# Layer two of a two-layer attention trunk: one 640-column score run a tile, two exponentials a tile, and bias tables laid out on the host

## The chip, the cores and the metric

The kernel runs on one core of one Trainium2 chip. The metric is the device time of one launch in microseconds, given as the median of several runs. On this core TensorE (PE) does the matrix products, VectorE (DVE) and ScalarE (ACT) do elementwise work and read PSUM, GpSimd (POOL) does elementwise work in SBUF alone, and SyncE (SP) issues nearly all DMA transfers in one queue.

## The reference, cut to what matters

Two layers run over 1024 latent tokens (a grid of 16 rows and 64 columns) and 256 context tokens, width 1024, 16 heads of 64. Layer one is grouped-query attention over all tokens. Layer two, which the change is about, lets each token see a window of 8 rows by 16 columns with a learned relative bias, and all 256 context tokens without bias:

```python
s_nb = einsum('bqhd,bqkhd->bhqk', qr, kw) * ATTN_SCALE + bias      # 8 x 16 window
s_cx = einsum('bqhd,bshd->bhqs', qr, kc) * ATTN_SCALE               # 256 context tokens
p = softmax(concatenate([s_nb, s_cx], axis=-1))
o = einsum('bhqk,bqkhd->bqhd', p[..., :n_nb], vw) + einsum('bhqs,bshd->bqhd', p[..., n_nb:], vc)
yx = (o * silu(z)) @ w_out
```

The output is `rms_norm(x + g_x * yx)`. The matrix products have to be better than fp16, so nearly every operand is split into a high and a low fp16 part.

## The kernel before

Tokens are stored column by column of the grid, so a tile of 128 tokens is 8 grid columns of 16 rows, and the window of a query tile t lies in the key tiles t-1, t and t+1. There are 8 latent tiles (`NX`) and 2 context tiles (numbers 8 and 9).

Layer two runs over 8 pairs of heads, u = 0 to 7. For a pair, `b_load(u)` fetches and splits weights, `b_qk(u)` and `b_vz(u)` project (tiles `pb` and `pvz`, L1360 and L1393/L1396), and `b_att(u)` does the attention. The projections of pair u+1 are interleaved with the attention of pair u, so that PE has work while the softmax of a tile is under way. After the last pair only `b_out` (tile `pob`, L1566, the output projection and the final norm) is left to interleave.

For each half of the latent tiles and each head of the pair, `b_att` goes through the query tiles two at a time:

- For each of the two tiles, the scores against the 2 or 3 near key tiles go to a PSUM bank of tag `st` (tile `bsn`, L1424 and L1425: two matmuls, for the high and low part of q). One custom DVE instruction (L1444) adds the bias table, writes `bpf` in SBUF and takes the row maximum.
- The scores of both tiles against the 256 context tokens go to one bank of tag `mx` (tile `bsc`), and one DVE reduction (L1451) takes their maxima. L1453 joins the two maxima, L1454 negates them and adds a constant.
- ACT computes four exponentials a tile: near and context in fp16 (L1462 and L1463, into `bph`), and near and context again in fp32 with row sums (L1464 and L1465, into `bpf`). The context ones read PSUM, so the `mx` bank is held until ACT is done with both tiles.
- `p_split` (L1042 on DVE for each second tile, L1045 on POOL for the others) subtracts to get the low part, a DMA transposes high and low (L1468, tile `bpht`), and later PE multiplies by v (L1473 and L1475, tile `bpv`).
- `fin` normalises four tiles at a time: L1484 adds the two row sums, L1485 and L1486 scale and invert them, L1488 copies one half of `bpv` out, L1489 adds the other half, and four instructions of L1491 multiply by the inverse sum and by the gate.

The bias tables are built on the chip. At the start of the kernel's life 16 small DMAs copy slices of the bias into DRAM (`toe`, L1318), 8 more spread them over 128 partitions (`tabd`, L1321). `b_table(h)` then loads 3 blocks of 128 columns for a head and POOL adds row masks with three instructions (L1333 to L1335), giving five blocks, of which a tile uses two or three.

PSUM has 8 banks: tags `pj`, `pv`, `st` and `mx`, two each. The order of instructions on every engine is not the order of the code. A `Planner` (a list scheduler with costs written by hand) lays out all instructions of the program, refines its order five times, and fixes it. It treats a PSUM tile as one resource, whatever part of it an instruction touches. A change in one place therefore moves instructions elsewhere too.

Of the kernel before, what the change touches and what calls it, by code (L numbers as in the profile page):

```python
# [40 lines left out]
PFB, PHB, PTB = 5, 5, 8  # L41
# [460 lines left out]
def trunk_kernel(ctx, tc, x, cx, cc, norm_g, ng_row, b_cols, sel_c, w_mod, w_mod0, b_mod, a_qz, a_kv, a_qg, a_kg, a_w_out,  # L502
                 b_in, rpb, b_w_out, fin_g, cos_t, sin_t, mask_q, out):
# [750 lines left out]
    def a_out(t, halves=(0, 1), tag="st"):  # L1254
# [13 lines left out]
        for hf in halves:  # L1268
            ps = psum.tile([P, 512], F32, name=f"poa{t}{hf}", tag=tag, bufs=2)
# [45 lines left out]
    toe = dram.tile([GR, NH, 31, GR], F32, name="toe")  # L1315
    for r in range(GR):
        a = bass.AP(rpb.tensor, rpb.offset + 15 - r, [[31 * 31, NH], [31, 31], [1, GR]])
        DM.dma_start(toe[r], a)  # L1318
    tabd = dram.tile([P, NH, 384], F32, name="tabd")
    for c in range(8):  # L1320
        DM.dma_start(tabd[c * GR:(c + 1) * GR],  # L1321
                     toe.rearrange("r h e k -> r h (e k)")[:, :, (7 - c) * GR:(7 - c) * GR + 384])
# [4 lines left out]
    def b_table(h):  # L1327

        tb = bl.tile([P, 5, P], F32, name=f"tb{h}", tag="tb", bufs=2)
        tabs[h] = tb  # L1330
# [3 lines left out]
        G.tensor_tensor(tb[:, 4], tb[:, 3], mq[:, 1], op=ALU.add)
# [77 lines left out]
    def b_att(u):  # L1412
# [14 lines left out]
        for hf in range(2):  # L1427
            og = bl.tile([P, 4, P], F32, name=f"bog{u}{hf}", tag="og", bufs=2)
            for i in range(2):
                tq = tabs[2 * u + i]  # L1430
                pv = psum.tile([P, 4, P], F32, name=f"bpv{u}{i}{hf}", tag="pv", bufs=2)
                sums = bl.tile([P, 4, 2], F32, name=f"bsm{u}{i}{hf}", tag="sums", bufs=2)
                for t0 in (hf * 4, hf * 4 + 2):
                    nm = f"{u}{i}{t0}"
                    near = {t: range(max(0, t - 1), min(NX, t + 2)) for t in (t0, t0 + 1)}
                    mx = bl.tile([P, 2, 2], F32, name="bmx" + nm, tag="bmx", bufs=3)
                    pfs = {}
                    for t in (t0, t0 + 1):
# [5 lines left out]
                        V.tensor_tensor_reduce(pfs[t][:, 0:n], st[:, 0:n * P].rearrange("p (a b) -> p a b", b=P), tsel,  # L1444
                                               op0=ALU.add, op1=ALU.max, scale=1.0, scalar=-3.0e38,
                                               accum_out=mx[:, t - t0, 0:1])
# [4 lines left out]
                    V.tensor_reduce(mx[:, :, 1], sx, axis=AX.X, op=ALU.max)  # L1451
# [1 line left out]
                    V.tensor_reduce(nmx, mx, axis=AX.X, op=ALU.max)  # L1453
                    V.tensor_scalar(nmx, nmx, -1.0, CSH, op0=ALU.mult, op1=ALU.add)  # L1454
                    for t in (t0, t0 + 1):
                        n, j, pf = len(near[t]), t - t0, pfs[t]
                        k_ = n + 2
                        pp = bl.tile([P, 10, P], F16, name=f"bph{u}{i}{t}", tag="ph", bufs=PHB)
# [3 lines left out]
                        S.activation(ph[:, 0:n], pf[:, 0:n], AF.Exp, bias=m)  # L1462
                        S.activation(ph[:, n:n + 2], cx_, AF.Exp, bias=m)  # L1463
                        S.activation(pf[:, 0:n], pf[:, 0:n], AF.Exp, bias=m, accum_out=sums[:, t % 4, 0:1])  # L1464
                        S.activation(pf[:, n:n + 2], cx_, AF.Exp, bias=m, accum_out=sums[:, t % 4, 1:2])  # L1465
# [13 lines left out]
                        yield 625  # L1479

                def fin(pv=pv, sums=sums, og=og, i=i, hf=hf):
                    nm = f"{u}{i}{hf}"
# [1 line left out]
                    V.tensor_reduce(sm, sums, axis=AX.X, op=ALU.add)  # L1484
# [3 lines left out]
                    S.copy(oc, pv[:, :, HD:P])  # L1488
                    V.tensor_tensor(oc, pv[:, :, 0:HD], oc, op=ALU.add)  # L1489
                    for t in range(4):  # L1490
                        V.scalar_tensor_tensor(og[:, t, i * HD:(i + 1) * HD], oc[:, t], sm[:, t:t + 1],  # L1491
                                               sz[:, hf * 4 + t, i * HD:(i + 1) * HD], op0=ALU.mult, op1=ALU.mult)
# [54 lines left out]
    def b_out(t, tag):  # L1547
# [39 lines left out]
def _tables():  # L1587
# [9 lines left out]
    p = np.arange(P)  # L1597
    c_, r_ = p // GR, p % GR
    r0 = np.clip(r_ - 4, 0, 8)
    rowok = (r_[None, :] >= r0[:, None]) & (r_[None, :] < r0[:, None] + 8)  # L1600
    lt = c_[None, :] < c_[:, None]
    q = np.stack([rowok & ~lt, rowok, rowok & lt], 1)
    import ml_dtypes
    m = lambda b: np.where(b, 0.0, NEG).astype(ml_dtypes.bfloat16)
    return lay(c64), lay(s64), m(q)
# [53 lines left out]
```

## Time and profile before

| | |
|---|---|
| median of 3 runs | 1364.47 us (1362.18 to 1364.70) |
| profiled execution, own time | 1365.58 us |
| its span (first to last instruction) | 1363.8 us |
| PE busy | 1329.9 us, 98% of the span |
| DVE, ACT, POOL busy | 1003.1, 910.2, 664.7 us (74%, 67%, 49%) |
| layer one, roughly | 100 to 690 us |
| layer two's projections and attention | 766 to 1300 us, one pair about 62 us |
| granted TensorE clock | 0.999 |

A row of a window table gives, for a stretch of time, each engine's busy time with the count of its instructions, in the order PE, weight loads, DVE, ACT, POOL, and then the granted clock, the busy share of the DMA engines and GB/s. What is missing from a window's length in the PE column is time in which PE had nothing it could run. A row of a group table gives line, engine, operation, tiles and shape, the count, and then busy time, mean length of one in ns, and the idle time just before with what ended it.

### The profile page before, as it was taken

What the parts mean: (1) busy time and instruction counts of PE and PEld (TensorE: products, weight loads), DVE (VectorE), ACT (ScalarE), POOL (GpSimd) and SP (SyncE); (2) the same over time, 40 slices, a digit from 0 to 9 for tenths busy, and PEclk for the clock granted to TensorE, in tenths of its full rate; (3) what the DMA queues carried; (4) which work ended last, traced back from release to release, by engine and by line L of the source; (5) the groups of instructions that cost most, each with busy time, mean ns of one, the idle gap of its engine ahead of it and who ended that gap; (6) DMA issues with size and microseconds to landing.
All of it is one profiled execution on the core that took longest, in us unless ns stands there. A gap on an engine that the chain in (4) does not pass through costs nothing.

```text
span 1363.8 us, 34709 instructions
## 1 busy us (share of the span) xinstructions
PE 1329.9 (98%) x13183; PEld 927.6 (68%) x13183; DVE 1003.1 (74%) x2647; ACT 910.2 (67%) x2186; POOL 664.7 (49%) x855
## 2 busy tenths in 40 slices
PE   9999999999999999999999999999999999999897
PEld 6457777777777777776554486777768686867543
DVE  5788788878788789887276846777776867777743
ACT  3653788888787876878632437777776777786711
POOL 2573787777778775788743201312222222332332
PEclk9999999999999999999999999999999999999999
DMA  9652577878789777847066725666576656677932
GB/s 352 186 162 76 108 145 156 154 161 166 149 152 169 146 150 138 172 145 210 10 171 175 178 80 120 125 132 138 117 153 110 156 96 146 113 159 141 194 101 102
DMA packets 426959, 198.23 MB, mean 145 GB/s; under 512 B 382560, under 2 KB 389664, under 8 KB 426792
## 3 DMA queue, kind: packets, MB, share of 16 engines
q1 hardware_dynamic: 426216, 195.98, 65.3%
q8 instruction: 103, 1.69, 0.5%
q14 instruction: 64, 0.52, 0.1%
q10 hardware_dynamic: 576, 0.03, 0.0%
HBM read 90.51 MB, written 15.22 MB: 78 GB/s over the span
## 4 chain that ended last, share of the span: by engine, by line
PE 68%; DVE 11%; ACT 9%; DMA 5%; POOL 3%; issue 3%; SPq 1%; DVEq 0%; POOLq 0%; ACTq 0%
PE pa L946 11%; PE pb L1360 9%; PE pvz L1393 9%; PE poa L1275 7%; PE pob L1566 6%; PE st L1183 2%; PE st L1184 2%; PE pkv L817 2%; ACT bpf L1464 2%; PE pm L976 2%; PE bpv L1473 1%; PE pv L1052 1%; PE qpv L1104 1%; PE pv L1053 1%; PE pv L1051 1%
## 5 line engine op out<-in xcount | busy, mean ns | idle before, releaser
L1045 POOL TENSOR_TENSOR pl<-pf,ph 128x256 f16<-128x256 f32 x340 | 234.1, 714 | 58.2 <-ACT pf L1170 44.5
L1045 POOL TENSOR_TENSOR bph<-bpf,bph 128x256 f16<-128x256 f32 (+1 forms) x128 | 99.9, 790 | 319.5 <-ACT bpf L1464 256.3
L946 PE MATMUL pa<-wa,x 128*128 128x256 f16 x1536 | 213.4, 272 | 0.1
L1360 PE MATMUL pb<-hb_hi,wb 128*128 128x512 f16 (+1 forms) x640 | 193.3, 358 | 1.4 <-DVE bk L1379 1.0
L1393 PE MATMUL pvz<-wb,hb_hi 128*128 128x256 f16 x1024 | 175.4, 273 | 0.6 <-DVE bk L1379 0.3
L946 PEld LDWEIGHTS <-x 128*128 128x128 f16 x1536 | 143.2, 97 | 35.7 <-issue 1.3
L1168 ACT ACTIVATE ph<-st 128x512 f16<-128x512 f32 x200 | 119.1, 604 | 60.7 <-PE st L1184 50.0
L1360 PEld LDWEIGHTS <-wb 128*128 128x128 f16 x960 | 92.7, 98 | 72.5 <-issue 2.9
L1393 PE MATMUL pvz<-wb,hb_lo 128*128 128x256 f16 x512 | 139.6, 273 | 0.0
L1170 ACT ACTIVATE pf<-st 128x512 f32<-128x512 f32 x200 | 119.3, 609 | 1.7 <-POOL pl L1045 1.6
L977 DVE TENSOR_REDUCE mxp<-pm 128x1 f32<-128x512 f32 x160 | 107.9, 684 | 13.7 <-PE pm L976 12.3
L1045 POOL TENSOR_TENSOR qpp<-qpf,qpp 128x512 f16<-128x512 f32 x84 | 97.9, 1186 | 38.4 <-ACT qpf L1127 32.2
L1360 PE MATMUL pb<-hb_lo,wb 128*128 128x512 f16 (+1 forms) x320 | 114.4, 358 | 0.0
L1393 PEld LDWEIGHTS <-hb_hi 128*128 128x128 f16 x1024 | 97.1, 98 | 24.2 <-DVE bk L1379 1.1
L1051 PE MATMUL pv<-v,ph 128*128 128x65 f16 x800 | 104.0, 193 | 0.2 <-ACT ph L1168 0.2
L1052 PE MATMUL pv<-v,ph 128*128 128x64 f16 x800 | 104.0, 195 | 0.0
L1053 PE MATMUL pv<-v,pl 128*128 128x65 f16 x800 | 101.4, 192 | 0.5 <-POOL pl L1045 0.5
L1566 PE MATMUL pob<-wob,ob 128*128 128x512 f16 x384 | 86.7, 379 | 2.6 <-DVE bmx L1444 0.9
L1051 PEld LDWEIGHTS <-ph 128*128 128x128 f16 x800 | 75.8, 97 | 19.0 <-ACT ph L1168 0.7
L1462 ACT ACTIVATE bph<-bpf,bnx 128x384 f16<-128x384 f32 (+1 forms) x128 | 68.7, 582 | 27.2 <-DVE bnx L1454 27.1
L1052 PEld LDWEIGHTS <-ph 128*128 128x128 f16 x800 | 75.5, 97 | 12.6
L1053 PEld LDWEIGHTS <-pl 128*128 128x128 f16 x800 | 76.1, 99 | 10.5 <-POOL pl L1045 1.6
(272 smaller groups left out, 3812.1 us busy)
## 6 DMA issues: line engine op xcount, KB each, us to landing
wg<-in_w_mod SPq DMA_DIRECT2D x64, 256.0 KB
wsb<-in_b_in SPq DMA_DIRECT2D x64, 256.0 KB
wm<-in_w_mod SPq DMA_DIRECT2D x16, 512.0 KB
wsa<-in_a_qz SPq DMA_DIRECT2D x32, 256.0 KB
xstage<-in_x SPq DMA_DIRECT2D x8, 512.0 KB
wsoa<-in_a_w_out SPq DMA_DIRECT2D x16, 256.0 KB
x<-in_x SPq DMA_DIRECT2D x8, 512.0 KB
x_d<-x SPq DMA_DIRECT2D x8, 512.0 KB
```

The source lines that it names most:

```text
L946: T.matmul(ps[:, :, i, :], hA(a, kt, t), wt[w][:, kt, :], start=n == 0, stop=n == 3 * KT - 1)
L977: V.tensor_reduce(mxs[i][:, t, ch:ch + 1], pm, axis=AX.X, op=ALU.max)
L1045: G.tensor_tensor(lo[:, c], p32[:, c], hi[:, c], op=ALU.subtract)
L1051: T.matmul(pv[:, t, :], hi[:, c], v[:, 0:65], start=first and t == 0, stop=False)
L1052: T.matmul(pv[:, t, 0:HD], hi[:, c], v[:, 65:129], start=False, stop=False)
L1053: T.matmul(pv[:, t, :], lo[:, c], v[:, 0:65], start=False, stop=last and t == n - 1)
L1168: S.activation(ph, st, AF.Exp)
L1170: S.activation(p32, st, AF.Exp)
L1275: T.matmul(ps, lhs(a, kt), w[b][:, kt, :], start=n == 0, stop=n == 3 * KT - 1)
L1360: T.matmul(ps[:, 0:n].rearrange("p (t q) -> p t q", q=P), wt[a][:, kt, which * P:(which + 1) * P], hb[b][:, c0 // P:(c0 + n) // P, kt], st ...
L1393: T.matmul(ps[:, :, j, :], hb[a][:, t, kt], wt[w][:, kt, 256:512], start=m == 0, stop=m == 3 * KT - 1)
L1566: T.matmul(ps, ob[kt][:, t // 4, a, c], wout["b"][hf][b][:, kt, :], start=n == 0, stop=n == 3 * KT - 1)
```

## The change

The near and context scores of a query tile now lie side by side in one PSUM tile of two banks (tag `db`, two of them, in place of `st` and `mx`), 640 columns, or 512 at the two ends of the grid. One DVE instruction adds a table that also covers the context columns (zeros there) and takes the maximum of all of them. L1451 and L1453 are gone. ACT computes two exponentials a tile, both from SBUF. The row sums are one number a tile, so L1484 is gone, and the end of `fin` is two multiplications of all four tiles instead of four instructions; these now work in place in PSUM.

The tables come as an input `tab` with nine blocks a head, masks and context zeros included, laid out on the host; `near(t)` picks five (or four) of the nine. The DMAs of `toe`, `tabd` and the mask, and POOL's three additions a head are gone.

For tile 0 the blocks are in another order (near, context, context, near), so that its scores take three runs of columns instead of two. `st` and `mx` lie in a PSUM pool of their own which closes before layer two's attention; layer one keeps its tags. The last four tiles of `b_out` use the `db` tag: both halves of a tile's output lie in one two-bank tile. `PTB`, the buffers for transposed probabilities, goes from 8 to 7. The weights of the interleaving (320, 320, 625, 625 a pair of tiles) become 540, 540, 405, 405, with the same sum.

```diff
-PFB, PHB, PTB = 5, 5, 8
+PFB, PHB, PTB = 5, 5, 7
...
-    toe = dram.tile([GR, NH, 31, GR], F32, name="toe")
-    for r in range(GR):
...
-        DM.dma_start(toe[r], a)
-    tabd = dram.tile([P, NH, 384], F32, name="tabd")
-    for c in range(8):
-        DM.dma_start(tabd[c * GR:(c + 1) * GR],
...
     def b_table(h):
-        tb = bl.tile([P, 5, P], F32, name=f"tb{h}", tag="tb", bufs=2)
...
-        DM.dma_start(flat, tabd[:, h])
-        G.tensor_tensor(tb[:, 0], tb[:, 1], mq[:, 1], op=ALU.add)
-        G.tensor_tensor(tb[:, 4], tb[:, 3], mq[:, 1], op=ALU.add)
-        G.tensor_tensor(tb[:, 1:4], tb[:, 1:4], mq, op=ALU.add)
+        tabs[h] = bl.tile([P, 9, P], F32, name=f"tb{h}", tag="tb", bufs=2)
+        DM.dma_start(tabs[h].rearrange("p a b -> p (a b)"), tab[h])
+
+    def near(t):
+        if t == 0:
+            return (0, NX, NX + 1, 1), ((0, 0, 1), (P, NX, 2), (3 * P, 1, 1)), slice(2, 9, 2)
+        if t == NX - 1:
+            return (t - 1, t, NX, NX + 1), ((2 * P, t - 1, 2), (4 * P, NX, 2)), slice(0, 7, 2)
+        return (t - 1, t, t + 1, NX, NX + 1), ((P, t - 1, 3), (4 * P, NX, 2)), slice(1, 6)
...
-                        st = ps_st(f"bsn{u}{i}{t}")
-                        scores(st[:, 0:n * P], i, t, slice(near[t][0] * P, (near[t][-1] + 1) * P))
-                        V.tensor_tensor_reduce(pfs[t][:, 0:n], ..., tsel, ..., accum_out=mx[:, t - t0, 0:1])
-                        yield 320
-                    sx = ps_mx(f"bsc{nm}", shape=(P, 2, 256))
-                    for j in range(2):
-                        scores(sx[:, j, :], i, t0 + j, slice(NX * P, TOK))
-                    V.tensor_reduce(mx[:, :, 1], sx, axis=AX.X, op=ALU.max)
+                        st = ps_db(f"bs{u}{i}{t}").rearrange("p a b -> p (a b)")
+                        for c, k0, n in parts:
+                            scores(st[:, c:c + n * P], i, t, slice(k0 * P, (k0 + n) * P))
+                        V.tensor_tensor_reduce(pfs[t][:, 0:k_], ..., tabs[2 * u + i][:, sel_t], ...,
+                                               accum_out=mx[:, t - t0:t - t0 + 1])
+                        yield 540
-                    V.tensor_reduce(nmx, mx, axis=AX.X, op=ALU.max)
...
-                        S.activation(ph[:, 0:n], pf[:, 0:n], AF.Exp, bias=m)
-                        S.activation(ph[:, n:n + 2], cx_, AF.Exp, bias=m)
-                        S.activation(pf[:, 0:n], pf[:, 0:n], AF.Exp, bias=m, accum_out=sums[:, t % 4, 0:1])
-                        S.activation(pf[:, n:n + 2], cx_, AF.Exp, bias=m, accum_out=sums[:, t % 4, 1:2])
+                        S.activation(ph, pf[:, 0:k_], AF.Exp, bias=m)
+                        S.activation(pf[:, 0:k_], pf[:, 0:k_], AF.Exp, bias=m, accum_out=sums[:, t % 4:t % 4 + 1])
...
-                        yield 625
+                        yield 405
...
-                    V.tensor_reduce(sm, sums, axis=AX.X, op=ALU.add)
...
-                    V.tensor_tensor(oc, pv[:, :, 0:HD], oc, op=ALU.add)
-                    for t in range(4):
-                        V.scalar_tensor_tensor(og[:, t, i * HD:(i + 1) * HD], oc[:, t], sm[:, t:t + 1],
-                                               sz[:, hf * 4 + t, i * HD:(i + 1) * HD], op0=ALU.mult, op1=ALU.mult)
+                    po = pv[:, :, 0:HD]
+                    V.tensor_tensor(po, po, oc, op=ALU.add)
+                    V.tensor_tensor(po, po, sums.unsqueeze(2).broadcast_to([P, 4, HD]), op=ALU.mult)
+                    V.tensor_tensor(og[:, :, i * HD:(i + 1) * HD], po, sz[:, hf * 4:hf * 4 + 4, ...], op=ALU.mult)
...
+    spool.close()
+    psum2 = ctx.enter_context(tc.tile_pool(name="psum2", bufs=2, space=PSUM))
+    def ps_db(name):
+        return psum2.tile([P, 2, 512], F32, name=name, tag="db", bufs=2)
...
         for hf in range(2):
-            ps = psum.tile([P, 512], F32, name=f"pob{t}{hf}", tag=tag, bufs=2)
+            if tag == "db" and hf == 0:
+                two = ps_db(f"pob{t}")
+            ps = two[:, hf] if tag == "db" else ps_tag(f"pob{t}{hf}", tag)
...
     for t in range(4, NX):
-        items.append((b_out(t, "st"), 7.35 + 0.25 * t, 7.6 + 0.25 * t, 10240))
+        items.append((b_out(t, "db"), 7.35 + 0.25 * t, 7.6 + 0.25 * t, 10240))
```

Three places show what the planner made of it, row by row. First ACT, in the attention of the last pair, the first two query tiles of its first head (`bpf` and `bph` are the probabilities in fp32 and fp16, `bsm` the row sums, `bnx` the negated maxima, `bv` and `pvz` belong to the projection). Before:

```order
L1462 ACTIVATE bph_21355<-bpf_21311,bnx_21352 128x256
L1462 ACTIVATE bph_21383<-bpf_21331,bnx_21352 128x384
L1464 ACTIVATE bpf_21311,bsm_21309<-bpf_21311,bnx_21352 128x256
L1463 ACTIVATE bph_21355<-bsc_21346,bnx_21352 128x256
L1464 ACTIVATE bpf_21331,bsm_21309<-bpf_21331,bnx_21352 128x384
L1465 ACTIVATE bpf_21311,bsm_21309<-bsc_21346,bnx_21352 128x256
L1403 CAST bv_20435<-pvz_21300 128x2x64
L1463 ACTIVATE bph_21383<-bsc_21346,bnx_21352 128x256
L1465 ACTIVATE bpf_21331,bsm_21309<-bsc_21346,bnx_21352 128x256
```

And the same two tiles now:

```order
L1455 ACTIVATE bph_20824<-bpf_20769,bnx_20822 128x512
L1455 ACTIVATE bph_20844<-bpf_20796,bnx_20822 128x640
L1456 ACTIVATE bpf_20769,bsm_20767<-bpf_20769,bnx_20822 128x512
L1477 COPY boc_20736<-bpv_20479 128x256
L1456 ACTIVATE bpf_20796,bsm_20767<-bpf_20796,bnx_20822 128x640
```

Eight exponentials became four, none of them reads PSUM, and the second tile's last one is the fifth row in place of the ninth.

Second PE, at the step from the first to the second half of the last output tile (`pob`; `wob` are weights, `ob` the attention's output). Before, the halves are two tiles (`pob_22458`, `pob_22486`). Here is the corresponding step one tile earlier, which reads the same way:

```order
L1566 LDWEIGHTS ob_21699
L1566 MATMUL pob_22388<-wob_20473,ob_21699 128x512
L1566 LDWEIGHTS ob_15149
L1566 MATMUL pob_22416<-wob_21316,ob_15149 128x512 [waits DVE_49]
L1566 LDWEIGHTS ob_15149
L1566 MATMUL pob_22416<-wob_21317,ob_15149 128x512
```

The last tile's step now:

```order
L1562 LDWEIGHTS ob_21122
L1562 MATMUL pob_21842<-wob_19993,ob_21122 128x512
L1562 LDWEIGHTS ob_15085
L1562 MATMUL pob_21842<-wob_20778,ob_15085 128x512 [waits DVE_49]
L1562 LDWEIGHTS ob_15085
L1562 MATMUL pob_21842<-wob_20779,ob_15085 128x512
```

Both halves are now in one tile, `pob_21842`, and the first matmul of the second half still waits for DVE. In the order before, the bank was last used two halves earlier, and that is the DVE read it waits for; now the last use of the tile ahead of it is DVE's read of the first half. In tiles 4, 5 and 6 the planner put six or more matmuls of another tile between the halves; in tile 7 there is none.

Third SP, some 50 us after the start (`wsa` are weights of layer one, `k_128`/`k_131` its keys). Before:

```order
L783 DMA gq<-in_a_qg 128x64
L1318 DMA toe<-in_rpb 496x16 x12
L873 DMA wsa_1310<-in_a_qz 128x512
L1318 DMA toe<-in_rpb 496x16
L831 DMA k_128<-k_128 64x4x128
L1318 DMA toe<-in_rpb 496x16 x3
```

Now:

```order
L788 DMA gq<-in_a_qg 128x64
L878 DMA wsa_1313<-in_a_qz 128x512
L836 DMA k_131<-k_131 64x4x128 x4
L878 DMA wsa_1341<-in_a_qz 128x512
L878 DMA wsa_1407<-in_a_qz 128x512
L836 DMA k_131<-k_131 64x4x128
```

The 24 issues for the tables are gone and the loads behind them move up. The rest of layer one has the same instructions in nearly the same order, with exchanges of neighbours on all engines.

More of the change, by code (lines that the diff above doesn't have):

```diff
@@ L510, in trunk_kernel, with ps_tag @@
     psum = ctx.enter_context(tc.tile_pool(name="psum", bufs=2, space=PSUM))
+    spool = ExitStack()
+    psum1 = spool.enter_context(tc.tile_pool(name="psum1", bufs=2, space=PSUM))
+    def ps_tag(name, tag, dt=F32, shape=(P, 512)):
+        return (psum if tag in ("pj", "pv") else psum1).tile(list(shape), dt, name=name, tag=tag, bufs=2)
     def ps_pj(name, dt=F32, shape=(P, 512)):
-        return psum.tile(list(shape), dt, name=name, tag="pj", bufs=2)
+        return ps_tag(name, "pj", dt, shape)
     def ps_mx(name, dt=F32, shape=(P, 512)):
-        return psum.tile(list(shape), dt, name=name, tag="mx", bufs=2)
+        return ps_tag(name, "mx", dt, shape)
     def ps_st(name):
-        return psum.tile([P, 512], F32, name=name, tag="st", bufs=2)
+        return ps_tag(name, "st")
     def ps_pv(name):
-        return psum.tile([P, 4, 65], F32, name=name, tag="pv", bufs=2)
+        return ps_tag(name, "pv", shape=(P, 4, 65))
     idf = main.tile([P, P], F32, name="idf")
@@ L834, in ps_kv @@
         tag = "mx" if t in () else ("st" if t % 4 < 2 else "pv")
-        return psum.tile([P, 512], F32, name=f"pkv{t}", tag=tag, bufs=2)
+        return ps_tag(f"pkv{t}", tag)
     mod_cols(0, wmp)
@@ L1268, in a_out @@
         for hf in halves:
[L1269 removed]
+            ps = ps_tag(f"poa{t}{hf}", tag)
             hc = slice(hf * 512, (hf + 1) * 512)
@@ L1429, in b_att @@
             for i in range(2):
-                tq = tabs[2 * u + i]
-                pv = psum.tile([P, 4, P], F32, name=f"bpv{u}{i}{hf}", tag="pv", bufs=2)
-                sums = bl.tile([P, 4, 2], F32, name=f"bsm{u}{i}{hf}", tag="sums", bufs=2)
+                pv = ps_tag(f"bpv{u}{i}{hf}", "pv", shape=(P, 4, P))
+                sums = bl.tile([P, 4], F32, name=f"bsm{u}{i}{hf}", tag="sums", bufs=2)
                 for t0 in (hf * 4, hf * 4 + 2):
                     nm = f"{u}{i}{t0}"
-                    near = {t: range(max(0, t - 1), min(NX, t + 2)) for t in (t0, t0 + 1)}
-                    mx = bl.tile([P, 2, 2], F32, name="bmx" + nm, tag="bmx", bufs=3)
-                    pfs = {}
+                    mx = bl.tile([P, 2], F32, name="bmx" + nm, tag="bmx", bufs=3)
+                    pfs, keys = {}, {}
@@ L1469, in b_att, with pvs @@
                         pht, plt = ppt[:, 0:k_], ppt[:, k_:2 * k_]
-                        def pvs(pv=pv, pht=pht, plt=plt, i=i, t=t, keys=list(near[t]) + [NX, NX + 1]):
+                        def pvs(pv=pv, pht=pht, plt=plt, i=i, t=t, keys=keys[t]):
                             for x_, kt in enumerate(keys):
@@ L1596, in _tables, with _bias @@
     lay = lambda a: np.ascontiguousarray(a.reshape(NX, P, HD).transpose(1, 0, 2)).astype(np.float32)
[L1597 to L1605, printed above, removed]
+    return lay(c64), lay(s64)
+def _bias(rpb):
+    rp = np.pad(rpb.transpose(0, 2, 1), ((0, 0), (0, 0), (8, 8)))
+    t = np.full((NH, P, 9, 8, GR), NEG, np.float32)
+    t[:, :, 4:8] = 0.0
+    for p in range(P):
+        c, r = divmod(p, GR)
+        k0 = min(max(r - 4, 0), 8)
+        k = slice(k0, k0 + 8)
+        v = rp[:, 7 - c:31 - c, 15 - r + k0:23 - r + k0]
+        t[:, p, 0, :, k], t[:, p, 8, :, k] = v[:, 0:8], v[:, 16:24]
+        t[:, p, 1, c:, k] = v[:, c:8]
+        t[:, p, 2, :, k] = v[:, 8:16]
+        t[:, p, 3, 0:c, k] = v[:, 16:16 + c]
+    return t.reshape(NH, P, 9 * P)
 def kernel(**inputs):
```

42 lines of the change are left out of this document (17 added, 25 removed).

## The prediction

> **What bounds the kernel now.** I read the page's busy shares first, then PE's busy time in stretches of 50 us, then the list of what PE waited for in layer two, then the groups of the instructions that change. The page's head and rows of the window table:
>
> ```profile
> span 1363.8 us, 34709 instructions
> PE 1329.9 (98%) x13183; PEld 927.6 (68%) x13183; DVE 1003.1 (74%) x2647; ACT 910.2 (67%) x2186; POOL 664.7 (49%) x855
> ...
> 50.00:100.00 50.00, 46.31 (x279) 25.99 (x277) 44.56 (x96) 32.83 (x74) 42.63 (x61) 1.00 0.50 128
> ...
> 300.00:350.00 50.00, 48.70 (x621) 37.39 (x620) 42.42 (x122) 41.47 (x85) 38.03 (x49) 1.00 0.87 164
> ...
> 950.00:1000.00 50.00, 49.89 (x502) 39.47 (x501) 35.36 (x109) 34.79 (x104) 12.61 (x18) 1.00 0.64 124
> ...
> 1200.00:1250.00 50.00, 46.84 (x460) 36.56 (x458) 34.94 (x107) 36.99 (x112) 16.18 (x22) 1.00 0.81 150
> 1250.00:1300.00 50.00, 45.85 (x387) 27.60 (x384) 38.85 (x112) 36.74 (x111) 17.57 (x19) 1.00 0.81 169
> 1300.00:1350.00 50.00, 50.00 (x247) 23.33 (x246) 17.94 (x39) 8.69 (x24) 16.55 (x17) 1.00 0.31 106
> ```
>
> From 850 to 1200 us PE has all the work it can do: 950 to 1000 is such a stretch, and it lacks 0.1 us of 50. Making DVE and ACT shorter there is worth next to nothing. Layer two loses PE time at one place, the end of the last pair, where no projection is left to interleave: 3.16 us in 1200 to 1250 and 4.15 us in 1250 to 1300, 7.3 us together. From 1300 on PE is full again. So the stretch 1200 to 1300 is the whole prize in layer two. What ended PE's waits from 780 us on:
>
> ```profile
> PE bsc L1424 <- ACT bpf L1465: 1.5, 1, 1.5
> PE bpv L1473 <- DMA bpht<-bph: 1.3, 1, 1.3
> PE pb L1360 <- DVE bk L1379: 1.0, 1, 1.0
> PE pob L1566 <- DVE bmx L1444: 0.9, 1, 0.9
> PE pob L1566 <- ACT wob L670: 0.7, 1, 0.7
> PE pob L1566 <- DVE wob L671: 0.6, 1, 0.6
> PE pb L1360 <- DVE bq L1375: 0.4, 2, 0.2
> PE bsn L1424 <- DVE bmx L1444: 0.4, 1, 0.4
> PE pob L1566 <- DVE bv L1404: 0.4, 1, 0.4
> ```
>
> Nearly all of it is DVE and ACT being late. Stretches of 20 us show how full they are:
>
> ```profile
> 1220.00:1240.00 20.00, 18.34 (x182) 14.90 (x181) 13.90 (x41) 13.81 (x43) 8.70 (x12) 1.00 0.63 118
> 1260.00:1280.00 20.00, 15.85 (x140) 9.69 (x139) 18.05 (x58) 19.97 (x61) 7.14 (x8) 1.00 0.94 203
> ```
>
> From 1260 to 1280 ACT is busy 19.97 us of 20 and DVE 18.05, and PE lacks 4.15 us there: the only place where the engines that the change relieves are the bound.
>
> **The change part by part.** The groups that it touches:
>
> ```profile
> L1465 ACT ACTIVATE bpf<-bsc,bnx 128x256 f32<-128x256 f32 x128 | 60.7, 474 | 0.5
> L1463 ACT ACTIVATE bph<-bsc,bnx 128x256 f16<-128x256 f32 x128 | 59.5, 467 | 0.2
> L1464 ACT ACTIVATE bpf<-bpf,bnx 128x384 f32<-128x384 f32 x96 | 58.5, 610 | 0.0
> L1462 ACT ACTIVATE bph<-bpf,bnx 128x384 f16<-128x384 f32 x96 | 55.5, 609 | 25.9 <-DVE bnx L1454 25.8
> L1444 DVE CUSTOM_DVE_ANT_0 bpf<-bsn,tb 128x384 f32<-128x384 f32 x96 | 53.0, 553 | 32.4 <-PE bsn L1425 29.3 <-POOL bph L1045 1.9
> L1451 DVE TENSOR_REDUCE bmx<-bsc 128x2 f32<-128x512 f32 x64 | 43.8, 684 | 5.1 <-PE bsc L1425 4.7
> L1491 DVE SCALAR_TENSOR_TENSOR bog<-boc,bse,bsz 128x64 f32<-128x64 f32 x128 | 37.2, 340 | 0.1
> L1465 ACT ACTIVATION_READ_ACCUMULATOR bpf<-bsc,bnx 128x1 f32 x128 | 26.3, 206 | 0.0
> L1464 ACT ACTIVATE bpf<-bpf,bnx 128x256 f32<-128x256 f32 x32 | 16.2, 506 | 0.0
> L1444 DVE CUSTOM_DVE_ANT_1 bpf<-bsn,tb 128x256 f32<-128x256 f32 x32 | 13.5, 423 | 6.0 <-POOL tb L1334 2.7 <-PE bsn L1425 1.6 <-issue 0.7
> L1489 DVE TENSOR_TENSOR boc<-bpv,boc 128x256 f32<-128x256 f32 x32 | 13.4, 419 | 24.0 <-ACT boc L1488 23.9
> L1453 DVE TENSOR_REDUCE bnx<-bmx 128x2 f32<-128x4 f32 x64 | 9.7, 152 | 0.7
> L1484 DVE TENSOR_REDUCE bse<-bsm 128x4 f32<-128x8 f32 x32 | 4.8, 152 | 0.0
> ```
>
> *ACT.* 384 columns take 610 ns and 256 take 506, so 128 more cost 104, and 640 columns 610 + 2 x 104 = 818. Four exponentials with one read of the sum each for the two in fp32 (the second read 206) cost 609 + 467 + 610 + 474 + 2 x 206 = 2572 ns a tile; two cost 2 x 818 + 206 = 1842. That is 0.73 us less a tile, 93 us over 128 tiles, and worth nothing from 850 to 1200 us, where PE is full.
>
> *DVE.* L1444 grows from 553 to 553 + 2 x 130 = 813 (130 is 553 less 423). A pair of tiles gains 2 x 260 and loses L1451's 684 and L1453's 152: 0.32 us less, 20 us in all. `fin` loses L1484 (152) and four of L1491 (1360) and gains two instructions of 256 elements in and out of PSUM. Layer one has the very same two forms:
>
> ```profile
> L1031 DVE TENSOR_TENSOR pv<-pv,ors 128x256 f32<-128x256 f32 x20 | 8.5, 425 | 0.2
> L1033 DVE TENSOR_TENSOR og<-pv,sz 128x256 f32<-128x256 f32 x20 | 8.3, 417 | 0.2
> ```
>
> So 842 replace 1512: 0.67 us less for each of 32. The `bpv` bank is held through two instructions more, 0.84 us; its reader has a second bank.
>
> *The end of the last pair.* The last pair has 16 tiles (two heads of eight) and four `fin`, so ACT has 16 x 0.73 = 12 us less to do there, DVE 16 x 0.16 + 4 x 0.67 = 5 us less. I go through PE's waits. The 1.5 us for L1465 goes with its cause: no ACT instruction holds a score bank any more. I leave 0.3 for a two-bank slot that is late: 1.2 gained. Waits that end on DVE (1.0, 0.9, 0.6, 0.4, 0.4, 0.4 and 0.6 in small ones not shown): 4.3 us. DVE loses 5 of the some 50 us that it works from 1220 to 1290 (near 14 in a quiet 20 us, 18 in the fullest), and besides its chain begins earlier because ACT no longer fills the stretch; I take 60%, 2.6 us. Late next is the splitting of weights (L671), which the change leaves alone. The 0.7 us for ACT's part of it I count as gained, since ACT loses 0.73 us for each tile of the fullest 20 us. Of the 1.3 us for a transposed tile 0.5: its DMA starts earlier, its time in the queue stays. Sum 5.0 us, between 1 (only the L1465 wait) and 7.3 (all).
>
> A page of the Trainium skill speaks against this step: "Perfetto Trace Analysis", section "Optimizing Scalar/DVE Operations", says that grouping into larger operations helps if the engine is saturated, and that breaking instructions up may let work finish sooner if it isn't but causes bubbles elsewhere. By the rows above the first case holds from 1260 to 1280, the second from 1220 to 1240 (13.81 and 13.90 of 20). What the second would cost is the rival on longer instructions below.
>
> *The last output tile.* Its two halves are now one tile, and the first matmul of the second half waits for DVE, with nothing of another tile left to put between. Two rows of the chain that ended last:
>
> ```profile
> 1304.08 51.81 PE pob L1566 x240
> 1355.92 0.70 DVE v L1570
> ```
>
> Matmuls follow each other at 51.81 / 240 = 0.216 us, and one is 0.38 long (the group of L1566 has a mean of 379 ns). From the last start to DVE is then 0.38 + 0.04, DVE takes 0.70, and about 0.05 brings it back: 1.17, less the 0.22 that the step takes anyway: a loss of 0.95, so 1.0 us. It lies on the path that ends the kernel and nothing hides it. It could be 0, if the wait shown is for an older read. The Trainium skill, "PSUM — Partial Sum Buffer", section "PSUM bank collisions raise a hardware error", gives as its rule to guard PSUM with semaphores "by bank × quadrant (by bank is the simple version), not by address". By that rule the halves, in two banks, need no such wait, and the sum would be 1.0 better; the order of the program has the wait, and I keep it.
>
> *PE's own work.* Tile 0 of each head has 2 x 3 score matmuls in place of 2 x 2. Two rows of the chain give the pitch of 256 and 128 columns:
>
> ```profile
> 811.11 2.68 PE pvz L1396 x48
> 979.85 2.62 PE pb L1360 x24
> ```
>
> Two of 256 take 2 x 0.109 = 0.218, four of 128 take 4 x 0.056 = 0.223: 0.1 us over 16 heads.
>
> *Tables.* POOL's 48 additions (29 us) go where POOL is busy 12.6 of 50 us. The DMA of a head's table grows from 192 to 576 KB, twice in 62 us; the DMA share of 0.64 has room, and its wait in SP's queue (for DVE's last use of the buffer) stands at the same place as before. Cost nothing; at worst transposes behind it are late by the 3 us that 576 KB take at the 203 GB/s of the row of 1260 to 1280, of which the four pending tiles would let through some 1 us. The 24 issues at the start:
>
> ```profile
> L1318 SPq DMA_DIRECT2D toe<-in_rpb x16: 490/622/1172, 47.5 to 65.1; - x16
> L1321 SPq DMA_DIRECT2D tabd<-toe x8: 599/617/1198, 68.0 to 77.9; - x8
> ```
>
> They take 15 us of SP's time between 47.5 and 78, behind which weights of layer one queue. PE lacks 3.7 us from 50 to 100, but POOL is busy 42.63 and DVE 44.56 of 50 there, and they, not SP, are late. I take 0.3 gained, between 0 and 2. `PTB` at 7 costs nothing as long as four tiles are pending (`BLAG`).
>
> *The planner.* Layer one's instructions swap neighbours. PE lacks 1.3 us of 50 there (the row of 300 to 350), some 12 us over all of layer one; that a new order moves this by an eighth, 1.5 us either way, is my estimate, taken as 0.
>
> *Sum.* -5.0 + 1.0 + 0.1 - 0.3 = -4.2 us. The profiled execution took 1365.58, so 1361.4 by it; it stood 1.1 above the median of 1364.47. Against the median: 1360.3 us.
>
> **The rivals.**
>
> 1. *Hidden after all.* The waits at the end are handed on: with DVE and ACT earlier, PE waits for the splitting of the output weights and for transposes (DMA share 0.94 from 1260 to 1280). Then only the L1465 wait and about 2 us more are won and 1.0 is lost at the last tile: a change of -2.7 to 0, some 1362.5 us. For it speaks that four different releasers stand in the list; against it that the most of them are DVE.
> 2. *Slower, by longer instructions on fewer slots.* A score slot is now held from the first near column to the end of an instruction of 813 + 82 ns; before, a near bank was free after 553. If DVE is late in the whole stretch 1220 to 1280, PE waits 0.26 us more for each of 16 tiles, 4.2 us, none of the 5.0 is won, and 1.0 is lost: 1364.47 + 5.3 = 1369.8. It decides once DVE has more work a tile than before; it has 0.16 us less, which speaks against.
> 3. *All of it.* PE's 7.3 us vanish, and the start gives 2: 1364.47 - 7.3 - 2 + 1.1 = 1356.3, and with luck in the order 1355.
> 4. *No change of the stretch.* The planner spends the room on another order of the same waits: 1364.5 to 1367. I count it with the first.
>
> **How the numbers follow.** About 0.2%, 2.7 us, can be told from no change. Chances: forecast (a gain of 2.8 to 6 us) 0.55, all of it (more than 6) 0.10, hidden or no change (within 2.7) 0.28, slower 0.07. Faster 0.65, same 0.28, slower 0.07. The time is the forecast's, 1360.3. The range reaches from the upper rival, 1356, to the far side of "no change", 1365; half of the third rival, the second and the part of "no change" above the old median are left out, some 0.2. A gain alone would give 1358.5 to 1361.7.
>
> **What would show it.** ACT busy about 35 of 50 us falls to 27 in layer two with PE unchanged at 49.9; the new exponential near 818 ns and L1444 near 813. PE busy 1200 to 1300 rises from 92.7 to some 97. One gap of about 1 us in PE some 5 us before its last matmul. If PE's waits between 1220 and 1290 add up to 5 us or more again, the step on the end of the pair is wrong; if layer one's end moves by over 1.5 us, the step on the planner is.

## The result, and the profile after

| | median (lowest to highest, runs) | ratio to before, 95% interval |
|---|---|---|
| before, in the same series | 1362.95 us (1361.61 to 1371.76, 16) | 1 |
| changed kernel | 1368.42 us (1363.92 to 1371.30, 16) | 1.0035 [1.0025, 1.0046] |

The change made the kernel slower by 0.35%, some 4.8 us. The forecast was 1360.3 us and its range ended at 1365. The profiled execution of the changed kernel took 1365.95 us, 2.5 below its median, while that of before (1365.58) lay 2.6 above the median here: the two traces tell where time went, and the timed runs tell how much. The runs below come from three more series on three chips; each ratio is to the kernel before in the same series.

The head of the page after, and the rows of its window table that answer to those shown of before:

```profile
span 1364.2 us, 34166 instructions
PE 1330.7 (98%) x13215; PEld 926.3 (68%) x13215; DVE 985.1 (72%) x2423; ACT 866.6 (64%) x1802; POOL 647.2 (47%) x807
...
50.00:100.00 50.00, 44.84 (x258) 23.89 (x257) 44.71 (x95) 32.10 (x74) 44.21 (x59) 1.00 0.19 55
...
300.00:350.00 50.00, 47.74 (x606) 36.13 (x604) 42.35 (x124) 41.39 (x85) 39.10 (x48) 1.00 0.88 157
...
950.00:1000.00 50.00, 49.71 (x466) 37.88 (x464) 34.61 (x82) 30.98 (x66) 9.48 (x12) 1.00 0.72 141
1200.00:1250.00 50.00, 49.51 (x481) 37.49 (x480) 36.04 (x92) 32.35 (x70) 13.27 (x14) 1.00 0.93 186
1250.00:1300.00 50.00, 48.35 (x416) 29.85 (x413) 38.36 (x89) 33.86 (x74) 18.91 (x21) 1.00 0.86 169
1300.00:1350.00 50.00, 49.87 (x233) 22.71 (x232) 16.64 (x34) 8.28 (x23) 15.84 (x16) 1.00 0.30 106
```

PE's lack from 1200 to 1300 went from 7.3 us to 0.49 + 1.65 = 2.1: the end of the last pair gives back 5.2 us, near the forecast of 5.0. But PE's lack from 50 to 100 grew from 3.7 to 5.2 us and from 300 to 350 from 1.3 to 2.3, in layer one, whose code nobody touched.

The first matmul of layer two's projections (`pb`, L1360) starts when PE is done with layer one, and the last `pob` ends layer two. So the two layers can be timed apart (starts in us, from the traces):

| | layer one ends | last `pob` | between them |
|---|---|---|---|
| before | 765.99 | 1355.50 | 589.5 |
| changed | 769.79 | 1355.79 | 586.0 |

Layer two became 3.5 us shorter; the sum had -5.0 + 1.0 + 0.1 = -3.9 for it. Layer one became 3.8 us longer.

What ended PE's waits in layer one (50 to 766 us), first before, then after (line numbers after are larger by 5 here):

```profile
PE st L1184 <- DMA q<-zt: 3.4, 3, 2.5
PE st L1183 <- ACT pf L1170: 2.1, 5, 0.7
PE pkv L817 <- DVE t2k L748: 1.3, 1, 1.3
PE qs L1116 <- DVE mxp L977: 1.3, 3, 0.5
...
PE qpv L1104 <- DMA qpt<-qpp: 0.6, 1, 0.6
```

```profile
PE st L1188 <- ACT pf L1175: 3.1, 6, 0.8
PE pm L981 <- DVE qmx L1124: 2.4, 3, 1.1
PE qpv L1109 <- DMA qpt<-qpp: 2.0, 3, 1.1
PE pkv L822 <- POOL x L817: 1.5, 2, 1.0
PE pv L1056 <- DVE og L1038: 1.5, 2, 1.1
PE pkv L822 <- DVE t2k L753: 1.3, 1, 1.3
PE pkt L832 <- POOL q16k L767: 1.3, 1, 1.3
...
PE po L1072 <- DVE og L1038: 0.8, 1, 0.8
```

No single wait carries the loss. But five of the rows belong to the new order: they stand in all four traces taken with it (`after`, and `a_again`, `rev` and `tonly` below), and are small or missing in the five with the old one. These are `pm` behind `qmx` (2.0 to 2.4 us in place of at most 0.4), `pv` behind `og` (1.5 for 0.2), `pkv` behind POOL's `x` (1.5 for at most 0.5), `pkt` (1.3 for 0) and `po` (0.8 for 0). A few small waits went away in exchange. The waits for DMA are no such mark: with the old order the `qpt` row alone is 0.6 us in one trace and 2.4 in another.

One of the five can be followed from row to row: the step at which PE transposes the last keys (`pkt`) before the projections `pa` begin. POOL, DVE and PE before, then after, from the timeline (start, duration, idle time before in brackets):

```profile
89.18 0.61 POOL L758 TENSOR_TENSOR t1k<-t1k,qrsk 128x256 f32<-128x256 f32 x1
90.31 0.90 POOL L762 TENSOR_TENSOR q16k<-t1k,q16k 128x256 f16<-128x256 f32 x1 [0.51 <-ACT q16k L761]
...
90.00 1.75 DVE L671 SCALAR_TENSOR_TENSOR wa<-wsa,wa 128x512 f16<-128x512 f32 x2
...
92.50 0.39 PE L827 MATMUL pkt<-id,q16k 128*128 128x128 f16 x4
...
94.89 3.33 PE L946 MATMUL pa<-wa,x 128*128 128x256 f16 x29
```

```profile
90.81 1.40 POOL L817 CAST xc_hi<-tf 128x256 f16<-128x256 f32 x2
92.17 0.78 POOL L763 TENSOR_TENSOR t1k<-t1k,qrsk 128x256 f32<-128x256 f32 x1
93.47 1.96 POOL L767 TENSOR_TENSOR q16k<-t1k,q16k 128x256 f16<-128x256 f32 x1 [0.51 <-ACT q16k L766]
...
93.61 1.28 DVE L676 SCALAR_TENSOR_TENSOR wa<-wsa,wa 128x512 f16<-128x512 f32 x2
...
95.48 0.40 PE L832 MATMUL pkt<-id,q16k 128*128 128x128 f16 x4 [1.26 <-POOL q16k L767]
...
97.01 1.25 PE L951 MATMUL pa<-wa,x 128*128 128x256 f16 x10
```

The chain that ends in `q16k` (multiply on POOL, cast on ACT, subtract on POOL) now comes behind two casts of `xc_hi`, 3.0 us later, and its last step takes 1.96 us in place of 0.90. In both kernels that step runs beside two DVE instructions for `wa`; before, those two took 1.75 us and POOL's step 0.90, after, they take 1.28 and POOL's step is the long one. PE waits 1.26 us, and `pa` starts 2.1 us later than before.

### The profile page after: what moved, and what is told of

The parts are those of the page before. It is cut to its first block, busy times and chain, and to the rows that moved or that the text cites. A ratio compares the mean times of both kernels' runs of the same rounds, so it can differ in the third digit from the quotient of the medians.

```text
span 1364.2 us, 34166 instructions
## 1 busy us (share of the span) xinstructions
PE 1330.7 (98%) x13215; PEld 926.3 (68%) x13215; DVE 985.1 (72%) x2423; ACT 866.6 (64%) x1802; POOL 647.2 (47%) x807
## 4 chain that ended last, share of the span: by engine, by line
PE 76%; DVE 9%; ACT 6%; DMA 4%; issue 3%; POOL 2%; SPq 0%; DVEq 0%; POOLq 0%; ACTq 0%
PE pa L951 13%; PE pb L1360 10%; PE pvz L1393 10%; PE poa L1280 7%; PE pob L1562 6%; PE st L1188 2%; PE st L1189 2%; PE pm L981 2%; PE bpv L1464 2%; PE bs L1424 2%; PE bs L1425 2%; PE pv L1057 2%; PE pvz L1396 2%; PE qs L1121 2%; PE pv L1058 2%
## 5 line engine op out<-in xcount | busy, mean ns | idle before, releaser
L1050 POOL TENSOR_TENSOR bph<-bpf,bph 128x256 f16<-128x256 f32 (+1 forms) x128 | 104.1, 835 | 404.7 <-issue 330.2
L1360 PE MATMUL pb<-hb_hi,wb 128*128 128x512 f16 (+1 forms) x640 | 192.7, 358 | 1.3 <-DVE bq L1375 1.3
L1360 PEld LDWEIGHTS <-wb 128*128 128x128 f16 x960 | 90.4, 98 | 71.0 <-DVE bq L1375 2.0
L1455 ACT ACTIVATE bph<-bpf,bnx 128x640 f16<-128x640 f32 (+1 forms) x128 | 98.3, 794 | 57.5 <-DVE bnx L1450 55.7
L1360 PE MATMUL pb<-hb_lo,wb 128*128 128x512 f16 (+1 forms) x320 | 114.5, 358 | 0.0
L1456 ACT ACTIVATE bpf<-bpf,bnx 128x640 f32<-128x640 f32 (+1 forms) x128 | 101.4, 793 | 1.5 <-DVE bpv L1480 0.8
L1056 PEld LDWEIGHTS <-ph 128*128 128x128 f16 x800 | 75.7, 96 | 20.0 <-issue 1.2
L1444 DVE CUSTOM_DVE_ANT_0 bpf<-bs,tb 128x640 f32<-128x640 f32 x96 | 78.5, 819 | 10.8 <-PE bs L1425 9.7
```

The lines of the kernel that those rows point to most:

```text
L1050: G.tensor_tensor(lo[:, c], p32[:, c], hi[:, c], op=ALU.subtract)
L1056: T.matmul(pv[:, t, :], hi[:, c], v[:, 0:65], start=first and t == 0, stop=False)
L1360: T.matmul(ps[:, 0:n].rearrange("p (t q) -> p t q", q=P), wt[a][:, kt, which * P:(which + 1) * P], hb[b][:, c0 // P:(c0 + n) // P, kt], st ...
L1456: S.activation(pf[:, 0:k_], pf[:, 0:k_], AF.Exp, bias=m, accum_out=sums[:, t % 4:t % 4 + 1])
```

## The experiments

The theory: the attention's change gains what the prediction said, and layer one loses more, because the planner, given 24 transfers fewer, wrote the rows of all engines in layer one in another order. Its rivals put the loss into layer two (longer instructions on fewer slots) or into the removed or enlarged transfers themselves.

**The two kernels once more** (`b_again`, `a_again`), unedited, to see how far a trace repeats.

> The kernel before, once more, for a second profile of it: the profile of before stood 2.6 us above the median of its runs, the profile of after 2.5 us below the median of its own. Theory A (what was lost was lost in layer one, by the order the planner wrote there): layer one ends earlier than in the first profile, its PE waits are 2 to 3 us smaller, and the pairs of layer two take 62.1 us as before. Rival B (the difference lies in layer two): layer one ends at 766 us again and layer two differs.

> The changed kernel, once more, for a second profile. Theory A: layer one ends later than 769.8 us in an ordinary run of 1368 us, and layer two takes the same 586 us from its first projection to its last matmul. Rival B: layer one ends at 770 us and layer two takes 2 to 3 us more than in the first profile.

Layer one ended at 765.51 and 769.98 us, layer two took 590.7 and 586.6: the split of the first two traces repeats within 1.2 us. The executions took 1366.25 and 1366.67 us. So Theory A's expectation that a second trace would show the larger loss of the timed runs was missed: layer one's end moved by 0.5 and 0.2 us only.

**The changed kernel with layer one's rows as before** (`pin`). The order that the planner found for layer one in the kernel before is written into the changed one, for PE, DVE, ACT, POOL and SP; the rows of layer two keep the order of the changed kernel.

```diff
         plan.refine(5, 100.0, 300.0)
+        _pin(plan)
...
+def _pin(plan):
+    for e, (n, txt) in _PIN.items():
...
+        have = set(ids.tolist())
+        rest = [(plan.start[i] + 97.5, i) for i in plan.order[e] if i not in have]
+        plan.order[e] = [i for _, i in heapq.merge(list(zip(tau.tolist(), ids.tolist())), rest, key=lambda p: p[0])]
```

> The changed kernel with layer one's instructions (all up to the first projection of layer two) in the order that the kernel before has, on all five engines; layer two as changed. Theory A: layer one as before, layer two 3.5 us shorter, so 3 to 4 us faster than before, ratio 0.9971 to 0.998. Rival B: as slow as the changed kernel, 4 to 5 us slower than before, ratio 1.003.

1362.1 us (1359.13 to 1363.86, 12 runs), ratio 0.9979 [0.9969, 0.999]: faster than before by 0.2%, and by 0.56% faster than the changed kernel with its 1.0035. Layer one ends at 764.97, layer two takes 586.8.

**The kernel before with layer one's rows as after** (`rev`), the same edit the other way round; the 24 table transfers stay in.

> The kernel before with layer one's instructions in the order that the changed kernel has (the 24 table DMAs stay where they were in time); layer two as before. Theory A: 4 us (by the two profiles) to 9 us (by the two medians, 5.5 + 3.5) slower than before, ratio 1.003 to 1.0065. Rival B: as fast as before, ratio 0.999 to 1.001.

1370.44 us (1370.22 to 1373.96, 6 runs), ratio 1.0047 [1.003, 1.0064]. Layer one ends at 772.05, layer two takes 591.8. With `pin` this makes a square:

| | layer one's order of before | layer one's order of after |
|---|---|---|
| attention before | 1 | 1.0047 [1.003, 1.0064] |
| attention after | 0.9979 [0.9969, 0.999] | 1.0035 [1.0025, 1.0046] |

The two effects multiplied give 0.9979 x 1.0047 = 1.0026, just inside the interval of both together. The order costs 0.47% with the attention before and 0.56% with that after; the attention's change gains 0.21% with the old order and 0.12% with the new.

**Only the transfers removed** (`tonly`): the kernel before, whose tables of three blocks a head come as an input.

```diff
-    toe = dram.tile([GR, NH, 31, GR], F32, name="toe")
-    for r in range(GR):
...
-        DM.dma_start(toe[r], a)
-    tabd = dram.tile([P, NH, 384], F32, name="tabd")
-    for c in range(8):
-        DM.dma_start(tabd[c * GR:(c + 1) * GR],
...
-        DM.dma_start(flat, tabd[:, h])
+        DM.dma_start(flat, tab3[h])
```

> The kernel before with one part of the change: the three bias blocks of a head come as an input, so the 24 DMAs of toe and tabd are gone; POOL's additions, the four exponentials and the score banks stay as before. The planner's order of layer one then is, row by row on every engine, that of the changed kernel. Theory A (removing 24 issues rewrites layer one's order, and that order is the loss): as slow as the run with layer one's order exchanged alone, 5 to 6 us slower than before, ratio 1.003 to 1.0065, layer one ending at 770 to 772 us. Rival (the issues gone are a saving or nothing, as the prediction had it, 0.3 us): ratio 0.999 to 1.0005.

1372.71 us (1370.82 to 1373.32, 6 runs), ratio 1.0064 [1.005, 1.0079]. Taking away 24 transfers, and nothing else, made the kernel 0.6% slower. The rows of layer one are here, one by one, those of the changed kernel, in the trace too. Layer one ends at 773.60, later than the 770 to 772 that were expected.

**The transfers put back** (`keep`): the changed kernel with the same 24 transfers issued as before, into DRAM that nobody reads.

```diff
+    toe = dram.tile([GR, NH, 31, GR], F32, name="toe")
+    for r in range(GR):
...
+        DM.dma_start(toe[r], a)
+    tabd = dram.tile([P, NH, 384], F32, name="tabd")
+    for c in range(8):
+        DM.dma_start(tabd[c * GR:(c + 1) * GR],
```

> The changed kernel with the 24 DMAs of toe and tabd put back, though nothing reads what they write; the attention is as changed. The planner's order of layer one then is, row by row, that of the kernel before. Theory A: 3 us faster than before, ratio 0.997 to 0.9985, layer one ending at 766 us. Rival (the gain of the pinned run needs the DMAs gone): 1 us or less faster, ratio 0.999 to 1.000.

1361.6 us (1360.34 to 1364.93, 12 runs), ratio 0.9986 [0.9974, 0.9998]. Useless work made the changed kernel faster by 0.5%, since with it the planner writes layer one's rows as in the kernel before. The ratio lies just outside of the expected 0.997 to 0.9985. Its window rows:

```profile
50.00:100.00 50.00, 46.04 (x271) 25.50 (x269) 45.57 (x96) 32.77 (x75) 42.49 (x60) 1.00 0.50 128
1200.00:1250.00 50.00, 49.33 (x515) 39.55 (x514) 34.80 (x91) 31.09 (x69) 12.71 (x15) 1.00 0.85 169
1250.00:1300.00 50.00, 48.41 (x373) 27.49 (x371) 36.93 (x85) 31.42 (x67) 18.15 (x20) 1.00 0.91 184
```

PE lacks 4.0 us from 50 to 100 (before 3.7, changed 5.2) at the DMA share 0.50 of before, and 2.3 us from 1200 to 1300. The 24 transfers themselves cost nothing that the runs show: `keep` and `pin` differ by 0.0007 in overlapping intervals.

**Only the first 105 us as before** (`pin100`): the edit of `pin`, but rows after 105 us are taken from the changed kernel's order.

> The changed kernel with only the first 105 us (as the planner counts them) in the order of the kernel before; the rest of layer one and layer two in the changed kernel's own order. By the two profiles 2.1 of layer one's 4.3 us are lost from 80 to 97 us, where PE waits for POOL (q16k), and the rest in small waits from 300 to 600 us. If the places add up: half of the loss comes back, 2 to 3 us slower than before, ratio 1.0012 to 1.0025. Rival (the later waits follow from the first one): ratio 0.997 to 0.999, as with all of layer one pinned.

1365.54 us (1363.54 to 1367.03, 12 runs), ratio 1.0012 [1.0003, 1.0021]. `pa` starts at 94.86 us again, so the 2.1 us at the start are back, and layer one ends at 768.15. From 1.0035 over 1.0012 to 0.9979 the start is worth 0.0023 and the rest of layer one 0.0033. Which is larger the intervals don't tell: the loss lies partly in the first 105 us and partly in the small waits after them.

**The last output tile's halves in two tiles** (`pinsep`): `pin`, and in the last four tiles of `b_out` each half takes a two-bank tile of its own.

```diff
-            if tag == "db" and hf == 0:
-                two = ps_db(f"pob{t}")
-            ps = two[:, hf] if tag == "db" else ps_tag(f"pob{t}{hf}", tag)
+            ps = ps_db(f"pob{t}{hf}")[:, 0] if tag == "db" else ps_tag(f"pob{t}{hf}", tag)
```

> The changed kernel with layer one in before's order, and the halves of the last four output tiles in two-bank tiles of their own, so that PE does not wait for DVE's read between the halves of the last one (a gap of 0.94 us in the profile of the changed kernel, 1.0 in the prediction). If that gap is on the path that ends the kernel: 0.9 us better than the pinned run, ratio 0.9965 to 0.998, and no gap in PE's last 10 us. If not: the ratio of the pinned run, 0.998, and the gap elsewhere.

1360.86 us (1359.38 to 1366.16, 12 runs), ratio 0.9982 [0.997, 0.9995], no different from `pin`. The wait at the last tile is gone, but another came some 19 us earlier. What ended PE's waits after 1300 us in `pin`, then in `pinsep`, and then DVE's row there in the timeline of `pinsep`:

```profile
PE pob L1562 <- DVE v L1566: 0.8, 1, 0.8
```

```profile
PE pob L1560 <- DVE v L1564: 1.3, 1, 1.3
```

```profile
1327.97 1.29 DVE L1564 TENSOR_TENSOR v<-pob,g 128x512 f32<-128x512 f32 x2 [4.53 <-DMA out<-v]
```

From start to start the two gaps cost 0.94 and 1.50 us. In `pinsep` DVE can't empty the PSUM tile because the SBUF buffer that it writes is still being sent out by the transfer of an earlier tile. So removing the wait did not pay, and its price of 1 us is measured in the trace alone.

**Two controls**: the kernel before with one number of the planner's refinement changed, 305 or 290 us in place of 300. No instruction is added or removed.

```diff
-        plan.refine(5, 100.0, 300.0)
+        plan.refine(5, 100.0, 305.0)
```

> The kernel before with one number of the planner changed: the refinement of the order looks at the first 305 us in place of 300. No instruction is added or taken away, nothing of layer two's code changes, but layer one's rows come in an order that is neither that of the kernel before nor that of the changed one. Theory (the order of layer one alone decides, and any small change of the planner's input reshuffles it): layer one's end, 765.5 to 766 us before, moves by 1 to 6 us in either direction, layer two keeps its 590 us, and the median follows, anywhere from 1358 to 1371. Rival (the order was harmed by the missing table transfers in particular, and a reshuffle as such is worth about nothing, as the prediction took it): layer one's end within 1.5 us of 766 and the median within 1.5 us of 1363.

> The same control with 290 us in place of 300. Theory: again another order, layer one's end moved by 1 to 6 us in either direction and not by the same amount as with 305; layer two 590 us; median anywhere from 1358 to 1371. Rival: layer one's end within 1.5 us of 766, median within 1.5 us of 1363.

With 305: 1367.49 us (1365.90 to 1369.02, 12 runs), ratio 1.0018 [1.0004, 1.0032], layer one ends at 769.65. With 290: 1369.42 us (1367.21 to 1372.62, 8 runs), ratio 1.0042 [1.0027, 1.0057], layer one ends at 774.01. Layer two takes 589.3 and 588.5. So it needs no lost transfer: a nudge of the planner's input costs 0.2 to 0.4%. With 290 layer one's end moved by 8 us, more than the 1 to 6 expected. All three other orders that were run (these two and that of the changed kernel) are slower than that of the kernel before.

## Why the prediction was wrong, point by point

- *The planner.* This is the step that failed: "that a new order moves this by an eighth, 1.5 us either way, is my estimate, taken as 0". The layer's end moved by 3.8 us in the first traces, 4.5 in the second, and in timed runs the order costs 0.0047 to 0.0064 of 1364 us, 6.4 to 8.7 us. It was sized as an eighth of PE's lack in that order (some 12 us), as if a new order could only shuffle the waits that were there; the list of waits after shows that another opens waits where there were none. Nor do the rows only "swap neighbours", as the prediction has it: when the traces of both kernels are matched by operation and tile names, the k-th of each with the k-th, 1013 of the first 1400 DVE instructions stand at another place, a tenth of them six or more places away and the farthest 28. The prediction also gave both signs the same weight. The controls speak against that, though three other orders are few: of four orders the one before is the best. That layer one's end moves by over 1.5 us was named as the sign of this failure; it had no rival with a chance of its own.
- *The start.* The 24 issues were "0.3 gained, between 0 and 2". By `keep` against `pin` they cost nothing that the runs show. What their removal did to the order is worth some 7 us, and the term had no room for it.
- *The end of the last pair.* Forecast 5.0 of 7.3 us, measured 5.2 (2.1 left); the L1465 wait is gone, and so is that for the transposed tile. The 4.3 us of waits for DVE held 0.5 that lie before 1200 us (one wait for `bq`, one for `bk`); in the stretch it was 3.8. The rule of the Trainium skill, "Perfetto Trace Analysis", section "Optimizing Scalar/DVE Operations", that grouping can help a saturated engine fits the 5.2 us here, where ACT was busy 19.97 of 20; no run separates the grouping from the rest of the attention's change. Its other case, in which breaking instructions up may let work finish sooner, may be the 1.3 us of waits for L1444 in the list below, which no run took apart.
- *The last output tile.* Forecast 1.0 us, measured 0.94, at 1349.67 us. That nothing hides it is not shown: `pinsep`, without it, was no faster than `pin`. The rule by bank of the Trainium skill, "PSUM — Partial Sum Buffer", section "PSUM bank collisions raise a hardware error", is not tested by this: the wait is put in by the program's order, tile by tile.
- *Layer two together.* Forecast -3.9, measured -3.5 and -4.1. `pin` puts it at 0.0021 x 1364 = 2.9 us in timed runs. Of the small terms one was missed: PE waits for `bq` in several pairs. All of PE's listed waits after 780 us:

```profile
PE pb L1360 <- DVE bq L1375: 1.3, 5, 0.3
PE bs L1424 <- DVE bmx L1444: 1.3, 4, 0.6
PE pob L1562 <- DVE v L1566: 0.8, 1, 0.8
PE pvz L1393 <- DVE bsz L1409: 0.4, 1, 0.4
PE pob L1562 <- DVE wob L676: 0.3, 1, 0.3
```

- *ACT's relief was mis-sized by half.* The durations were right (818 forecast):

```profile
L1456 ACT ACTIVATE bpf<-bpf,bnx 128x640 f32<-128x640 f32 x96 | 78.7, 820 | 1.2 <-DVE bpv L1480 0.8
L1444 DVE CUSTOM_DVE_ANT_0 bpf<-bs,tb 128x640 f32<-128x640 f32 x96 | 78.5, 819 | 10.8 <-PE bs L1425 9.7
L1456 ACT ACTIVATION_READ_ACCUMULATOR bpf<-bpf,bnx 128x1 f32 x128 | 24.1, 188 | 0.0
```

  But instructions that follow each other without a wait overlap on ACT, as the starts in the timeline show. Before, and then after:

```profile
1262.13 0.63 ACT L1464 ACTIVATE bpf<-bpf,bnx 128x384 f32<-128x384 f32 x1
1262.64 0.22 ACT L1464 ACTIVATION_READ_ACCUMULATOR bpf<-bpf,bnx 128x1 f32 x1
1262.73 0.49 ACT L1463 ACTIVATE bph<-bsc,bnx 128x256 f16<-128x256 f32 x1
1263.09 0.65 ACT L670 ACTIVATE wob<-wsob 128x512 f16<-128x512 f32 x1
```

```profile
1266.78 0.82 ACT L1456 ACTIVATE bpf<-bpf,bnx 128x640 f32<-128x640 f32 x1
1267.50 0.19 ACT L1456 ACTIVATION_READ_ACCUMULATOR bpf<-bpf,bnx 128x1 f32 x1
1267.59 1.14 ACT L675 ACTIVATE wob<-wsob 128x512 f16<-128x512 f32 x2
```

  An exponential of 384 columns takes 0.51 us from its start to the next, one of 256 takes 0.36, a read 0.09, one of 640 columns 0.72. A tile therefore went from 2 x 0.51 + 2 x 0.36 + 2 x 0.09 = 1.92 us to 2 x 0.72 + 0.09 = 1.53: 0.39 us less, where the prediction had 0.73. The page agrees: ACT's busy time fell by 43.6 us, 0.34 for each of 128 tiles, not by 93. For the same reason ACT in 950 to 1000 fell to 30.98, not 27. DVE's relief came out smaller too: the terms add up to some 41 us, and its busy time fell by 18.0. There, four instructions of L1491 in a row took 0.87 us in the timeline and not 1.36, and the subtraction described at the end took 5.8 us more. The gain on PE came out right all the same, so that 5.0 met 5.2 is in part luck.

## What to carry to other kernels

Where a planner lays out a whole program, price the re-plan itself: an edit that only takes transfers away cost 0.6% here, and the order that was there when this kernel was tuned was better than each of the three others that were run, which is few for a rule. Keep the order outside of the changed part fixed (here `pin`, 0.9979, or `keep`, 0.9986, both faster than before) and time the change on that; the version with the tables as an input and layer one's old order beats both kernels. And take an engine's relief from start to start in the timeline, not from the mean length of an instruction.

## What the runs showed that was not expected

- *One 128x640 subtraction costs more after the change.* `p_split` on DVE, same line, shape and types, before and after:

```profile
L1042 DVE TENSOR_TENSOR bph<-bpf,bph 128x640 f16<-128x640 f32 x48 | 39.4, 821 | 16.0 <-ACT bpf L1465 15.7
```

```profile
L1047 DVE TENSOR_TENSOR bph<-bpf,bph 128x640 f16<-128x640 f32 x48 | 45.2, 942 | 21.9 <-ACT bpf L1456 18.7 <-DMA bpht<-bph 2.9
```

  `rev` has 821 and `keep` 942, so it goes with the attention's code, not with layer one's order. The mean hides two cases. In the changed kernel's trace 31 of the 48 take 0.80 to 0.83 us, much as before. The other 17 begin while a subtraction of POOL on its own `bph` still runs, take 0.88 to 1.29 us, and every one of them ends 0.68 us after POOL's. Before, none begins beside such a subtraction. One of each, and PE 2.4 us after the end of the second:

```profile
897.14 0.83 DVE L1047 TENSOR_TENSOR bph<-bpf,bph 128x640 f16<-128x640 f32 x1
...
901.34 1.30 POOL L1050 TENSOR_TENSOR bph<-bpf,bph 128x256 f16<-128x256 f32 x2 [5.83 <-issue]
902.05 1.27 DVE L1047 TENSOR_TENSOR bph<-bpf,bph 128x640 f16<-128x640 f32 x1 [2.93 <-ACT bpf L1456]
...
905.74 0.39 PE L1360 MATMUL pb<-hb_hi,wb 128*128 128x512 f16 x1 [0.26 <-DVE bq L1375]
```

  So the long ones go with POOL's subtraction, by up to 0.47 us each; no run moved the two apart. It costs DVE 5.8 us in all. What it costs PE is open: each of the five waits for `bq` (1.3 us together, the term that was missed above) ends 3.7 us after the start of such a long subtraction, with the instructions that make `bq` behind it on DVE.
- *One order, several times.* With layer one's rows as before its end lay at 765.99, 765.51, 764.97, 763.95 and 762.90 us in five traces; with those of after at 769.79, 769.98, 772.05 and 773.60 in four. Runs of the kernel before and of the changed one spread over 7 us and more. Why the changed kernel's two traces lie 2 us below its median is open: they put the difference between the kernels at 0.4 us, the runs put it at 4.8.
